# Third projection chunk with row blocks outermost, the token permutation beside it, and modulation sums two steps later

## The chip, the cores and the metric

The kernel runs on one core of a Trainium2 chip, as one launch. A core has TensorE (PE in the profile, with its weight loads as PEld), VectorE (DVE), ScalarE (ACT), GpSimd (POOL) and SyncE (SP, which here issues nearly all DMAs). Each engine works through its own queue in order and waits on semaphores for the others. The metric is device microseconds (us) of one execution, as the median of several runs; lower is better. A difference of under 0.2% (about 5.5 us here) is what a measurement of this kernel can't tell from no change.

## The reference

Two transformer-like blocks in float32 on 1024 tokens of width 1024 (8 tiles of 128 tokens), the first with 256 context tokens beside them (2 tiles). Only the head of the first block matters here:

```
mod   = silu(c) @ w_mod + b_mod                  # 6 x 1024 values
h     = rms_norm(x)   * norm1 * (1 + sc1) + sh1  # 1024 tokens
hc    = rms_norm(ctx) * norm1 * (1 + csc1) + csh1  # 256 context tokens
q_a, k_a, v_a, q_b, k_b, v_b = split(h @ w_in)   # and of hc @ w_in: k and v
q_a, k_a = rope(rms_norm(q_a)), rope(rms_norm(k_a))
q_b, k_b = rms_norm(q_b), rms_norm(k_b)
o_a = window attention(q_a, k_a, v_a, context)
o_b = 2-D neighbourhood attention(q_b, k_b, v_b, context)   # 16 rows x 64 columns of tokens
```

After it come the output projection, a gated feed-forward layer, a gated linear attention block and a second feed-forward layer with a convolution; none of these is touched.

## The kernel before, in words

Matrix products keep float32 accuracy by splitting each operand into a rounded part `hi` and a rest `lo` and adding three products: hi x whi, hi x wlo, lo x whi (`mm3`, lines 233 to 238; the loads of `hi`, `lo` are the stationary side, 128 x 128, and 256 weight columns stream through). The normalized tokens lie in `hT` (a `hi` and a `lo` tile, each 8 row blocks of 128 features x 1024 tokens) and those of the context in `hc`.

`w_in` is worked in nine chunks of 256 columns, list `P1C` (line 310), here called chunk 0 (`kva`), 1 and 2 (`qa`), 3 (`vb`), 4 and 5 (`kb`), 6 and 7 (`qb`), 8 (`vb`). The loop of lines 781 to 804 goes over chunks 2 to 8 and, inside, over token tiles `t`; `project` (line 716) runs 24 matmuls for one tile (8 row blocks x 3) into one of four PSUM buffers `acc`, and `evac` has ScalarE copy the sums to SBUF (line 629 or 617) and take four sums of squares of 64 columns (line 632). Beside each tile step three kinds of work are issued:

- `W.tick()` splits one quarter of the next chunk's weights (line 139 on ScalarE, 140 on VectorE) and, after the fourth, issues the next load;
- `do_later(2)` takes two items from the list `later`: for a chunk of queries or keys that is one `rsqrt` (11 small VectorE instructions, lines 248 to 261), and for each pair of tiles a `gain` (line 647 on VectorE, 649 on GpSimd), for `kva` and `qa` a `turn` (rotation, lines 518 to 523 on GpSimd and VectorE), and a `store` (a DMA, line 606);
- `mod_use()` adds one of 32 row blocks of `w_mod`, times one value of silu(c), to a sum `macc` on VectorE (lines 555, 557) and issues the load of a later block into one of three buffers `mraw` (line 537). Eight row blocks make one group of 1024 modulation values. With the next call after the eighth, `mod_row` has TensorE add `macc` over its 128 partitions (`pm`, line 580, two issues of 512 columns), VectorE add the bias (line 581), and with the call after that the row is stored.

Chunks 0 to 2 use the tokens in natural order. From chunk 3 on they must stand in strips of 8 columns of the 16 x 64 grid. `to_strips` (line 701), called between chunks 2 and 3, permutes `hT` in place: for each row block, ScalarE copies `hi` to an `mraw` buffer (line 709), GpSimd copies `lo` to a spare buffer (line 712), and VectorE writes both back in the new order (line 713, 16 instructions). Chunk 3 begins with the two context tiles, which are not permuted. SP issues the DMAs in program order; a spill that waits for a `turn` holds up the `mraw` loads behind it.

Of the kernel before, what the change touches and what calls it, by code (L numbers as in the profile page):

```python
# [9 lines left out]
F32 = mybir.dt.float32  # L10
R32 = mybir.dt.float32r
I32 = mybir.dt.int32
AF = mybir.ActivationFunctionType
# [5 lines left out]
P = 128  # L19
D = 1024  # L20
KD = 8
S = 1024
# [190 lines left out]
def kernel(ctx: ExitStack, tc: tile.TileContext, a: dict, out: bass.AP, dbg=None):  # L213
    nc = tc.nc
# [309 lines left out]


    mods = [(j, k) for j in range(4) for k in range(8)]
    mst = {"load": 0, "use": 0, "raw": {}}
    mpl = {}

    def mod_load():  # L530
# [8 lines left out]

    def mod_use():  # L540
        i = mst["use"]
        if i >= 34:
            return
        mst["use"] += 1
        for f in mst.pop("next", []):
            f()
        if i >= 32:
            return
        j, k = mods[i]
        r = mst["raw"].pop(i)  # L550
        if k == 0:
            mst["acc"] = mpl["p"].tile([P, 1024], F32, tag="macc", name="macc", bufs=2)
        m = mst["acc"]
        if k == 0:
            nc.vector.tensor_scalar(out=m, in0=r, scalar1=sil[:, k:k + 1], scalar2=None, op0=ALU.mult)
        else:
            nc.vector.scalar_tensor_tensor(
                out=m, in0=r, scalar=sil[:, k:k + 1], in1=m, op0=ALU.mult, op1=ALU.add)
        mod_load()
        if k == 5:  # L560
            mst["row"] = [mod_row_load(j, half) for half in range(2)]
        if k == 7:
            rows_ = mst.pop("row")
            mst["next"] = [lambda half=half: mod_row(j, half, m, rows_[half]) for half in range(2)]

    def row_view(n, k):
        o_ = voff[n] + k
# [6 lines left out]
            nc.sync.dma_start(out=row[:, 2], in_=row_view("norm2", 4 * half))  # L574
        return row

    def mod_row(j, half, m, row):
        c = slice(half * 512, half * 512 + 512)
        pm = ps_m.tile([P, 512], F32, tag="misc", name="pm", bufs=2)
        nc.tensor.matmul(pm[0:1, :], one1, m[:, c], start=True, stop=True)  # L580
        nc.vector.tensor_tensor(out=row[:, 0], in0=pm[0:1, :], in1=row[:, 1], op=ALU.add)
        if j == 2:
            nc.vector.scalar_tensor_tensor(out=row[:, 0], in0=row[:, 0], scalar=1.0,
                                           in1=row[:, 2], op0=ALU.add, op1=ALU.mult)

        def store():
            nc.sync.dma_start(out=dmod[j, c].rearrange("(o n) -> o n", o=1), in_=row[:, 0])

        mst.setdefault("next", []).append(store)

    def lhs(nm, t, k):
        if t >= 8:
            return [hc[i][:, k, (t - 8) * P:(t - 7) * P] for i in range(2)]
        return [hT[i][:, k, t * P:(t + 1) * P] for i in range(2)]
# [10 lines left out]
    def spill(dd, t, half, src):  # L605
        nc.sync.dma_start(out=dd[t:t + 2, :, half * 256:half * 256 + 256].rearrange("t p c -> p t c"), in_=src)

    def evac(ci, t, ps):
        nm, c0 = P1C[ci]
        half = {"kb": (c0 - 1280) // 256, "vb": (c0 - 1792) // 256, "qa": c0 // 256,  # L610
                "qb": (c0 - 768) // 256, "kva": 0}[nm]
        e = t % 2
        if nm == "vb":
            if e == 0:
                raws["v"] = p1.tile([P, 2, 256], F32, tag="vt", name="vt", bufs=2)
            vt = raws["v"]
            nc.scalar.activation(out=vt[:, e], in_=ps[:, :256], func=AF.Copy)
            if e == 1:
                spill(dvb, t - 1, half, vt)
            return  # L620
        nh = 2 if nm == "kva" else 4
        w = nh * 64
        nt_ = 10 if nm[0] == "k" else 8
        if t == 0:
            ss = p1.tile([P, 2, 40], F32, tag="hss", name="hss", bufs=4)
            raws[ci] = (KA if nm == "kva" else (p1 if ci in (1, 4, 6) else mpl["p"]).tile(
                [P, 10, 256], F32, tag="raw", name="raw"), ss)
        x, ss = raws[ci]
        nc.scalar.activation(out=x[:, t], in_=ps[:, 0:w], func=AF.Copy)
        for h in range(nh):  # L630
            sq = p1.tile([P, 64], F32, tag="hsq", name="hsq", bufs=2)
            nc.scalar.activation(out=sq, in_=ps[:, h * 64:h * 64 + 64], func=AF.Square,
                                 accum_out=ss[:, 0, t * nh + h:t * nh + h + 1])
        if nm == "kva":
            pv = ps[:, 128:256].rearrange("p (h d) -> p h d", h=2)
            nc.scalar.activation(out=VA[:, t, :, 0:64], in_=pv, func=AF.Copy)
            nc.vector.tensor_tensor(
                out=VA[:, t, :, 64:128], in0=pv, in1=VA[:, t, :, 0:64].bitcast(F32), op=ALU.subtract)
        if t < nt_ - 1:
            return  # L640
        gi = {"kva": 1, "kb": 3, "qa": 0, "qb": 2}[nm]
        last = {}

        def gain(t0):
            xx = x[:, t0:t0 + 2].rearrange("p t (h d) -> p (t h) d", d=64)
# [12 lines left out]
        def store(t0):  # L658
            src = last.get(t0, x[:, t0:t0 + 2])
            if nm == "kva":  # L660
                nc.vector.tensor_copy(out=x[:, t0:t0 + 2], in_=src)
            else:
                spill({"qa": dqa, "qb": dqb, "kb": dkb}[nm], t0, half, src)

        later.append(lambda: rsqrt(p1, ss[:, 1, :nt_ * nh], ss[:, 0, :nt_ * nh], nt_ * nh, 1.0 / 64))
        stages = [gain, turn, store] if nm in ("kva", "qa") else [gain, store]
        for i in range(nt_ // 2 + len(stages) - 1):
            for j, f in reversed(list(enumerate(stages))):
                t0 = 2 * (i - j)
# [28 lines left out]
            eng = nc.vector if t < 2 else nc.gpsimd  # L698
            eng.tensor_tensor(out=lo, in0=src, in1=hi.bitcast(F32), op=ALU.subtract)

    def to_strips():

        spare = p1.tile([P, 10, 256], F32, tag="raw", name="raw").rearrange("p a b -> p (a b)")
        for k in range(8):
            for i in range(2):
                h = hT[i][:, k]
                if i == 0:
                    tmp = mpl["p"].tile([P, 1024], F32, tag="mraw", name="mraw", bufs=3)
                    nc.scalar.activation(out=tmp, in_=h.bitcast(F32), func=AF.Copy)
                else:  # L710
                    tmp = spare[:, k % 2 * S:k % 2 * S + S]
                    nc.gpsimd.tensor_copy(out=tmp, in_=h.bitcast(F32))
                nc.vector.tensor_copy(out=h.rearrange("p (s r c) -> p s r c", s=8, c=8),  # L713
                                      in_=tmp.rearrange("p (r s c) -> p s r c", s=8, c=8))

    def project(ci, t):
        nm, c0 = P1C[ci]
        wi, wl = map(kc8, W.slots(ids["in", ci]))
        ps = ps_a.tile([P, 512], F32, tag="acc", name="pin", bufs=4)
        mm3(ps[:, :256], [(*lhs(nm, t, k), wi[:, k], wl[:, k]) for k in range(8)])  # L720
        evac(ci, t, ps)

# [58 lines left out]
    for ci, (nm, c0) in enumerate(P1C):  # L781
        if ci < 2:
            continue
        W.get(ids["in", ci])
        if ci == 3:
            to_strips()
            for _ in range(3):
                mod_load()
        ts = list(range(10 if nm in ("kb", "vb") else 8))
        for t in ts[8:] + ts[:8] if ci == 3 else ts:  # L790
            project(ci, t)
            if t >= 1:
                W.tick()
            do_later(2)
            if ci > 3 - (t > 1) and (t % 4 != 3 or ci == len(P1C) - 1):
                mod_use()
            if ci == len(P1C) - 1 and t == 5:
                do_later(99)
                while mst["use"] < 34:
                    mod_use()  # L800
                st_mod.close()
                qp = pool("q_raw", "left", stack=st_o)
                for x in range(3):
                    load_q(x)
# [1375 lines left out]
```

## Time and profile before

| | us |
|---|---|
| median of 3 runs | 2749.98 (2746.62 to 2752.45) |
| the profiled execution's own time | 2745.07 |
| its span on the core | 2743.1 |
| TensorE busy | 2583.6 (94% of the span) |
| VectorE busy | 1713.6 (62%) |
| ScalarE busy | 1053.2 (38%) |
| GpSimd busy | 1186.5 (43%) |

The projection stage lies between about 112 and 346 us of the span; the change is in it. TensorE is busy nearly throughout the kernel, so the places where it waits are looked for. Times in rows count from the start of the span. A matmul row's duration is that of its whole passage; matmuls overlap, and from one start to the next is the pace. A value in square brackets is idle time of the engine before the row, with what ended it. PEclk is the granted TensorE clock as a share of its upper level: 1.00 is 2.4 GHz, 0.50 is 1.2 GHz.

### The profile page before, as it was taken

To read this page: it belongs to the slowest core of one execution; us is meant where nothing else is said; L and a number is where in the kernel's file an instruction comes from. 1 tells how busy PE (TensorE), PEld (TensorE's weight loads), DVE (VectorE), ACT (ScalarE), POOL (GpSimd) and SP (SyncE) were. 2 spreads that over 40 slices of the span, in tenths; PEclk is the share of its full clock that TensorE was granted. 3 is DMA by queue.
4 is the path that set the end of the run, shared out by engine and by line. 5 is a ranking of instruction groups with operands and counts; after the bars stand their busy time and mean duration, and the time that the engine had idled before them with its cause. 6 is when DMAs were issued, how large, how long until landed. Compare 5 with 4: busy or idle time off the path is not lost. (4 is left out here: it accounts for less than half of the span.)

```text
span 2743.1 us, 37060 instructions
## 1 busy us (share of the span) xinstructions
PE 2583.6 (94%) x13861; PEld 2143.0 (78%) x13861; DVE 1713.6 (62%) x3361; ACT 1053.2 (38%) x2605; POOL 1186.5 (43%) x1079
## 2 busy tenths in 40 slices
PE   8969988888989999999999999999999999999998
PEld 4968977777987788888887868778777777777786
DVE  4585589999465555555564632422677777777766
ACT  4524377777232222222222542422443333333333
POOL 2462246677344677766662312121433333333321
PEclk9989999999999999999999999999999999999999
DMA  6145422220211111112112111111101111111112
GB/s 238 55 131 175 156 58 53 67 73 13 101 39 47 46 47 46 47 47 62 47 46 70 35 46 31 47 31 47 39 31 47 47 47 46 47 52 52 48 49 85
DMA packets 152540, 170.85 MB, mean 62 GB/s; under 512 B 39444, under 2 KB 135460, under 8 KB 151336
## 3 DMA queue, kind: packets, MB, share of 16 engines
q1 hardware_dynamic: 152200, 168.35, 19.4%
q8 instruction: 109, 1.79, 0.3%
q0 software_dynamic: 160, 0.14, 0.1%
q14 instruction: 71, 0.58, 0.1%
HBM read 154.81 MB, written 13.65 MB: 61 GB/s over the span
## 5 line engine op out<-in xcount | busy, mean ns | idle before, releaser
L140 POOL TENSOR_TENSOR wlo<-raw,whi 128x512 fp32r<-128x512 f32 x132 | 179.3, 1363 | 449.1 <-ACT whi L139 420.3
L1635 PE MATMUL pgu<-h,whi 128*128 128x512 f32 x864 | 342.4, 396 | 3.1 <-DVE h L1571 3.1
L1636 PE MATMUL pgu<-h,wlo 128*128 128x512 f32 x864 | 341.0, 395 | 0.5 <-POOL wlo L140 0.5
L1634 PE MATMUL pgu<-h,whi 128*128 128x512 f32 x864 | 341.3, 395 | 0.0
L140 DVE TENSOR_TENSOR wlo<-raw,whi 128x512 fp32r<-128x512 f32 (+2 forms) x304 | 232.2, 776 | 165.0 <-ACT whi L139 164.1
L139 ACT ACTIVATE whi<-raw 128x512 fp32r<-128x512 f32 (+1 forms) x436 | 232.2, 551 | 173.0 <-DMA raw<-in_w_down 60.9
L1653 DVE TENSOR_TENSOR uv<-pgu,uv 128x512 f32<-128x512 f32 x216 | 148.2, 686 | 149.8 <-PE pgu L1636 128.7
L237 PE MATMUL pdn<-wlo,hid 128*128 128x512 f32 x576 | 227.4, 395 | 12.3 <-DVE wlo L140 12.3
L236 PE MATMUL pdn<-whi,hid 128*128 128x512 f32 x576 | 226.5, 393 | 1.5 <-DVE uv L1362 1.1
L238 PE MATMUL pdn<-whi,hid 128*128 128x512 f32 x576 | 226.7, 394 | 0.0
L1363 POOL TENSOR_TENSOR x<-x,uv 128x512 f32<-128x512 f32 x144 | 192.2, 1356 | 31.6 <-DVE uv L1362 28.8
L1635 PEld LDWEIGHTS pgu<-h,whi 128*128 128x128 f32 x864 | 162.2, 188 | 42.2 <-DVE h L1571 3.6
L1634 PEld LDWEIGHTS pgu<-h,whi 128*128 128x128 f32 x864 | 162.4, 188 | 40.0
L1636 PEld LDWEIGHTS pgu<-h,wlo 128*128 128x128 f32 x864 | 162.2, 188 | 39.9 <-POOL wlo L140 0.9
L1504 POOL TENSOR_TENSOR hid<-sg,hid 128x512 fp32r<-128x512 f32 x80 | 106.9, 1341 | 193.7 <-ACT hid L1503 191.7
L1656 POOL TENSOR_TENSOR uv<-uv 128x512 f32<-128x512 f32 x72 | 106.2, 1475 | 163.8 <-DVE uv L1653 163.8
L236 PE MATMUL pin<-whi,h 128*128 128x256 f32 x576 | 167.5, 291 | 8.4 <-ACT whi L139 3.5
L238 PE MATMUL pin<-whi,h 128*128 128x256 f32 x576 | 168.1, 292 | 6.3 <-DVE h L713 6.1
L237 PE MATMUL pin<-wlo,h 128*128 128x256 f32 x576 | 166.7, 289 | 2.1 <-DVE wlo L140 2.1
L237 PEld LDWEIGHTS pdn<-wlo,hid 128*128 128x128 f32 x576 | 108.1, 188 | 41.9 <-DVE wlo L140 17.4
L1503 ACT ACTIVATE hid<-sg 128x512 fp32r<-128x512 f32 x80 | 50.3, 632 | 231.6 <-DVE sg L1501 231.6
L236 PEld LDWEIGHTS pdn<-whi,hid 128*128 128x128 f32 x576 | 108.2, 188 | 28.0 <-DVE uv L1362 1.5
(381 smaller groups left out, 7048.2 us busy)
## 6 DMA issues: line engine op xcount, KB each, us to landing
raw<-in_ffn_w_up SPq DMA_DIRECT2D x22, 1024.0 KB, 5.2
mraw<-in_w_mod SPq DMA_DIRECT2D x32, 512.0 KB, 4.1
raw<-in_w_gate SPq DMA_DIRECT2D x11, 1024.0 KB, 5.3
raw<-in_w_up SPq DMA_DIRECT2D x11, 1024.0 KB, 5.5
raw<-in_w_down SPq DMA_DIRECT2D x11, 1024.0 KB, 4.9
raw<-in_ffn_w_down SPq DMA_DIRECT2D x11, 1024.0 KB, 5.0
raw<-in_w_in SPq DMA_DIRECT2D x9, 1024.0 KB, 5.3
wm<-in_w_mod SPq DMA_DIRECT2D x8, 1024.0 KB, 13.1
```

The lines of the kernel that those rows point to most:

```text
L139: nc.scalar.activation(out=hi, in_=src, func=AF.Copy)
L140: (engine or self.engine or nc.vector).tensor_tensor(out=lo, in0=src, in1=hi.bitcast(F32), op=ALU.subtract)
L236: nc.tensor.matmul(ps, lh, rh, start=(i == 0), stop=False)
L237: nc.tensor.matmul(ps, lh, rl, start=False, stop=False)
L238: nc.tensor.matmul(ps, ll, rh, start=False, stop=(i == n - 1))
L1363: nc.gpsimd.tensor_tensor(out=xs, in0=xs, in1=tmp, op=ALU.add)
L1504: nc.gpsimd.tensor_tensor(out=hl[:, c], in0=sg[:, cc, c], in1=hh[:, c].bitcast(F32), op=ALU.subtract)
L1634: nc.tensor.matmul(ps, lh, rh, start=start and k == 0, stop=False)
L1635: nc.tensor.matmul(ps, lh, rl, start=False, stop=False)
L1636: nc.tensor.matmul(ps, ll, rh, start=False, stop=stop and k == n - 1)
L1653: nc.vector.tensor_tensor(out=o, in0=ps, in1=u, op=ALU.add)
L1656: nc.gpsimd.tensor_tensor(out=o, in0=u, in1=v, op=ALU.add)
```

## The change

It has four parts.

1. Chunk 2 no longer goes tile by tile. `to_strips(ci)` runs it with the row block `k` outermost: four PSUM buffers hold the sums of all eight tiles (two tiles per buffer), and for each `k` all eight tiles get their three matmuls. Before them ScalarE copies both parts of row block `k` into `mraw` buffers (three in all), and after them VectorE writes both back in strip order, so that row block `k` is permuted once chunk 2 has read it. GpSimd's copies and their spare buffer are gone. One weight quarter (from k = 1) and one `later` item are issued per `k`. After k = 7 all eight tiles are evacuated; their sums of squares become eight `later` items, read from SBUF.
2. In chunk 3 the two context tiles use the PSUM buffers `tp` (`early`) instead of `acc`.
3. `mod_use` is called in three of five tile steps instead of three of four.
4. `mod_row` runs with the second `mod_use` call after the group's last addition instead of the next one, and its store with the fourth instead of the second.

```
-        for f in mst.pop("next", []):
+        for f in mst["next"].pop(i, []):
...
-            mst["next"] = [lambda half=half: mod_row(j, half, m, rows_[half]) for half in range(2)]
+            mst["next"][i + 2] = [lambda half=half: mod_row(j, half, m, rows_[half], i + 4) for half in range(2)]
...
-    def to_strips():
+    def to_strips(ci):
+        wi, wl = map(kc8, W.slots(ids["in", ci]))
+        pss = [ps_a.tile([P, 512], F32, tag="acc", name="pin", bufs=4) for _ in range(4)]
+        pss = [pss[t // 2][:, t % 2 * 256:t % 2 * 256 + 256] for t in range(8)]
         for k in range(8):
+            tmp = []
             for i in range(2):
+                tmp.append(mpl["p"].tile([P, 1024], F32, tag="mraw", name="mraw", bufs=3))
+                nc.scalar.activation(out=tmp[i], in_=hT[i][:, k].bitcast(F32), func=AF.Copy)
+            for t in range(8):
+                hi, lo = lhs(P1C[ci][0], t, k)
+                nc.tensor.matmul(pss[t], hi, wi[:, k], start=(k == 0 and t % 2 == 0), stop=False)
+                nc.tensor.matmul(pss[t], hi, wl[:, k], start=False, stop=False)
+                nc.tensor.matmul(pss[t], lo, wi[:, k], start=False, stop=(k == 7 and t % 2 == 1))
+            for i in range(2):
+                nc.vector.tensor_copy(out=hT[i][:, k].rearrange("p (s r c) -> p s r c", s=8, c=8),
+                                      in_=tmp[i].rearrange("p (r s c) -> p s r c", s=8, c=8))
+            if k >= 1:
+                W.tick()
+            do_later()
+        for t in range(8):
+            evac(ci, t, pss[t], True)
...
-        if ci == 3:
-            to_strips()
+        if ci == 2:
+            to_strips(ci)
             for _ in range(3):
                 mod_load()
+            continue
...
-            if ci > 3 - (t > 1) and (t % 4 != 3 or ci == len(P1C) - 1):
+            if t % 5 in (0, 2, 4) or ci == len(P1C) - 1:
                 mod_use()
```

What moves, engine by engine. On TensorE the place is chunk 2; `pin` with a number is one PSUM buffer. Before, the end of its first tile and the begin of the second:

```order
L237 MATMUL pin_1237<-wlo_66,h1_0_279 128x256
L238 MATMUL pin_1237<-whi_65,h1_1_280 128x256
L236 MATMUL pin_1288<-whi_65,h1_0_279 128x256
L237 MATMUL pin_1288<-wlo_66,h1_0_279 128x256
L238 MATMUL pin_1288<-whi_65,h1_1_280 128x256
```

Now, the end of the first row block and the begin of the second:

```order
L723 MATMUL pin_1240<-whi_65,h1_1_280 128x256
L721 MATMUL pin_1237<-whi_65,h1_0_279 128x256
L722 MATMUL pin_1237<-wlo_66,h1_0_279 128x256
L723 MATMUL pin_1237<-whi_65,h1_1_280 128x256
L721 MATMUL pin_1238<-whi_65,h1_0_279 128x256
```

A buffer stood for 24 matmuls in a row before; now for 6 (the row for 1237 covers two tiles, each with its three), and all four are open until the chunk's end. The number of matmuls is the same.

On VectorE the place is the permutation; a CAST writes one part of one row block. Before, the last two of sixteen that stand in one block, and what follows:

```order
L713 CAST h_0_279<-mraw 128x1024
L713 CAST h_1_280<-raw 128x1024
L140 TENSOR_TENSOR wlo<-raw,whi 128x512
L647 TENSOR_TENSOR KA<-KA,hss 128x256
L661 COPY KA<-qr 128x256
L555 TENSOR_SCALAR macc<-mraw,sil 128x1024
```

Now, the two casts of one row block in chunk 2, between a `turn` and the next split and `gain`:

```order
L522 TENSOR_TENSOR qr<-raw,rope 128x8x16
L523 TENSOR_TENSOR qr<-qr,rp_1360 128x8x16
L725 CAST h_0_279<-mraw 128x1024
L725 CAST h_1_280<-mraw 128x1024
L140 TENSOR_TENSOR wlo<-raw,whi 128x512
L654 TENSOR_TENSOR raw<-raw,hss 128x512
```

The casts moved from one block between chunks 2 and 3 into pairs inside chunk 2, and both now read what ScalarE copied.

On TensorE the second place is the first modulation sum in chunk 4. Before, behind the tile of step t = 2:

```order
L238 MATMUL pin_2230<-whi_65,h1_1_280 128x256
L580 MATMUL pm_2266<-macc_1725,ones_72 1x512
L580 MATMUL pm_2269<-macc_1725,ones_72 1x512
L236 MATMUL pin_2276<-whi_65,h1_0_279 128x256
L237 MATMUL pin_2276<-wlo_66,h1_0_279 128x256
```

Now, behind the tile of step t = 5:

```order
L238 MATMUL pin_2286<-whi_65,h1_1_280 128x256
L580 MATMUL pm_2323<-macc_1657,ones_72 1x512
L580 MATMUL pm_2326<-macc_1657,ones_72 1x512
L236 MATMUL pin_2332<-whi_65,h1_0_279 128x256
L237 MATMUL pin_2332<-wlo_66,h1_0_279 128x256
```

The last addition to the group's `macc` was issued in step t = 1 of chunk 4 before, one tile ahead of the sum, and is in step t = 2 now, three tiles ahead. The other three sums moved in the same way: behind step t = 9 of chunk 5, t = 4 of chunk 7 and t = 5 of chunk 8 (before: t = 2 of chunk 5, t = 2 of chunk 6, t = 5 of chunk 7).

## Rows read from the trace of the kernel before

**Rows 1.** The page, section 1: busy time, share of span, instructions.

```profile
PE 2583.6 (94%) x13861; PEld 2143.0 (78%) x13861; DVE 1713.6 (62%) x3361; ACT 1053.2 (38%) x2605; POOL 1186.5 (43%) x1079
```

**Rows 2.** Waits of TensorE from 110 to 360 us: total, times, longest.

```profile
PE pm L580 <- DVE macc L557: 20.3, 4, 12.1
PE pin L238 <- DVE h L713: 6.1, 7, 2.2
```

**Rows 3.** Windows: stretch, its us, busy per engine (instructions), PEclk, DMA share, GB/s.

```profile
161.30:168.10 6.80, 6.74 (x29) 6.34 (x30) 6.66 (x21) 0.38 (x1) 0.91 (x2) 0.50 0.71 210
193.80:205.90 12.10, 0.00 (x0) 0.00 (x0) 10.80 (x18) 1.72 (x10) 10.26 (x14) 0.71 0.50 160
205.90:209.30 3.40, 3.37 (x5) 0.38 (x5) 1.25 (x2) 0.00 (x0) 0.00 (x0) 0.54 0.70 207
209.30:237.90 28.60, 28.60 (x241) 28.43 (x240) 14.61 (x23) 12.38 (x84) 3.15 (x2) 1.00 0.44 145
237.90:241.50 3.60, 0.04 (x1) 0.00 (x0) 3.60 (x5) 1.72 (x10) 2.31 (x2) 1.00 0.90 269
241.50:243.30 1.80, 1.75 (x4) 0.25 (x4) 1.80 (x2) 0.00 (x0) 1.12 (x1) 1.00 0.77 153
```

**Rows 4.** Timeline of TensorE around its two longest waits: start, us, what.

```profile
143.00 0.28 PE L238 MATMUL pin<-whi,hc 128*128 128x256 f32 x1
146.39 0.39 PE L236 MATMUL pin<-whi,h 128*128 128x256 f32 x1 [3.11 <-DVE h L713]
149.07 0.58 PE L238 MATMUL pin<-whi,h 128*128 128x256 f32 x1 [2.19 <-DVE h L713]
...
193.51 0.28 PE L238 MATMUL pin<-whi,h 128*128 128x256 f32 x1
205.93 3.41 PE L580 MATMUL pm<-macc,ones 128*1 128x512 f32 x4 [12.13 <-DVE macc L557]
```

**Rows 5.** Timeline of TensorE in chunk 2's first tile (granted clock 0.50).

```profile
114.03 0.41 PE L238 MATMUL pin<-whi,h 128*128 128x256 f32 x1
...
116.59 0.41 PE L238 MATMUL pin<-whi,h 128*128 128x256 f32 x1
```

**Rows 6.** Lines of the permutation: ns min/median/max, first and last start us.

```profile
L713 DVE CAST h<-mraw x8: 675/678/824, 145.5 to 161.2; 128x1024 fp32r<-128x1024 f32 x8
L713 DVE CAST h<-raw x8: 679/1522/1524, 147.5 to 161.8; 128x1024 fp32r<-128x1024 f32 x8
L709 ACT ACTIVATE mraw<-h x8: 1056/1058/1087, 138.7 to 155.8; 128x1024 f32<-128x1024 f32 x8
```

**Rows 7.** Timeline of VectorE: a root, a gain, a turn, a modulation step.

```profile
114.87 0.17 DVE L248 TENSOR_SCALAR rs_v<-hss 128x32 f32<-128x32 f32 x1
117.33 0.69 DVE L647 TENSOR_TENSOR raw<-raw,hss 128x512 f32<-128x512 f32 x1
...
164.71 0.68 DVE L140 TENSOR_TENSOR wlo<-raw,whi 128x512 fp32r<-128x512 f32 x1
...
180.49 0.69 DVE L647 TENSOR_TENSOR raw<-raw,hss 128x512 f32<-128x512 f32 x1
182.66 0.29 DVE L521 TENSOR_TENSOR rp<-raw,rope 128x128 f32<-128x128 f32 x1 [1.48 <-POOL raw L649]
184.95 1.48 DVE L557 SCALAR_TENSOR_TENSOR macc<-mraw,sil,macc 128x1024 f32<-128x1024 f32 x1
...
204.60 1.27 DVE L557 SCALAR_TENSOR_TENSOR macc<-mraw,sil,macc 128x1024 f32<-128x1024 f32 x1
```

**Rows 8.** Timeline of GpSimd: the last instruction of chunk 2's last turn.

```profile
204.07 0.46 POOL L520 TENSOR_TENSOR qr<-qr,rp 128x128 f32<-128x128 f32 x1
```

**Rows 9.** Timeline of ScalarE: one tile's evacuation, then a split.

```profile
129.12 0.39 ACT L629 ACTIVATE raw<-pin 128x256 f32<-128x256 f32 x1 [1.12 <-PE pin L238]
...
130.18 0.66 ACT L139 ACTIVATE whi<-raw 128x512 fp32r<-128x512 f32 x1
```

**Rows 10.** Timeline of SP: the first loads of queries for the attention stage.

```profile
335.73 3.16 SPq L778 DMA_DIRECT2D qraw<-dqa  x6
```

More of the change, by code (lines that the diff above doesn't have):

```diff
@@ L526 @@
     mods = [(j, k) for j in range(4) for k in range(8)]
-    mst = {"load": 0, "use": 0, "raw": {}}
+    mst = {"load": 0, "use": 0, "raw": {}, "next": {}}
     mpl = {}
@@ L541, in mod_use @@
         i = mst["use"]
-        if i >= 34:
+        if i >= 36:
             return
         mst["use"] += 1
-        for f in mst.pop("next", []):
+        for f in mst["next"].pop(i, []):
             f()
@@ L575, in mod_row_load, with mod_row @@
         return row
-    def mod_row(j, half, m, row):
+    def mod_row(j, half, m, row, at):
         c = slice(half * 512, half * 512 + 512)
@@ L587, in store @@
             nc.sync.dma_start(out=dmod[j, c].rearrange("(o n) -> o n", o=1), in_=row[:, 0])
-        mst.setdefault("next", []).append(store)
+        mst["next"].setdefault(at, []).append(store)
     def lhs(nm, t, k):
@@ L606, in spill, with evac @@
         nc.sync.dma_start(out=dd[t:t + 2, :, half * 256:half * 256 + 256].rearrange("t p c -> p t c"), in_=src)
-    def evac(ci, t, ps):
+    def evac(ci, t, ps, put_off=False):
         nm, c0 = P1C[ci]
@@ L629, in evac, with squares @@
         nc.scalar.activation(out=x[:, t], in_=ps[:, 0:w], func=AF.Copy)
[L630 to L633, printed above, removed]
+        def squares(src):
+            for h in range(nh):
+                sq = p1.tile([P, 64], F32, tag="hsq", name="hsq", bufs=2)
+                nc.scalar.activation(out=sq, in_=src[:, h * 64:h * 64 + 64], func=AF.Square,
+                                     accum_out=ss[:, 0, t * nh + h:t * nh + h + 1])
+        if put_off:
+            later.append(lambda: squares(x[:, t]))
+        else:
+            squares(ps)
         if nm == "kva":
@@ L699, in h_fm @@
             eng.tensor_tensor(out=lo, in0=src, in1=hi.bitcast(F32), op=ALU.subtract)
-    def to_strips():
-        spare = p1.tile([P, 10, 256], F32, tag="raw", name="raw").rearrange("p a b -> p (a b)")
+    def to_strips(ci):
+        wi, wl = map(kc8, W.slots(ids["in", ci]))
+        pss = [ps_a.tile([P, 512], F32, tag="acc", name="pin", bufs=4) for _ in range(4)]
+        pss = [pss[t // 2][:, t % 2 * 256:t % 2 * 256 + 256] for t in range(8)]
         for k in range(8):
+            tmp = []
@@ L705, in to_strips @@
             for i in range(2):
[L706 to L714, printed above, removed]
@@ L716, in project @@
-    def project(ci, t):
+                tmp.append(mpl["p"].tile([P, 1024], F32, tag="mraw", name="mraw", bufs=3))
[5 more added lines that the diff above has]
+                nc.tensor.matmul(pss[t], lo, wi[:, k], start=False, stop=(k == 7 and t % 2 == 1))
@@ L717, in project @@
+            for i in range(2):
[6 more added lines that the diff above has]
+            evac(ci, t, pss[t], True)
+    def project(ci, t, early=False):
         nm, c0 = P1C[ci]
         wi, wl = map(kc8, W.slots(ids["in", ci]))
-        ps = ps_a.tile([P, 512], F32, tag="acc", name="pin", bufs=4)
+        if early:
+            ps = ps_t.tile([P, 512], F32, tag="tp", name="pin", bufs=2)
+        else:
+            ps = ps_a.tile([P, 512], F32, tag="acc", name="pin", bufs=4)
@@ L784 @@
         W.get(ids["in", ci])
-        if ci == 3:
-            to_strips()
+        if ci == 2:
+            to_strips(ci)
             for _ in range(3):
                 mod_load()
+            continue
         ts = list(range(10 if nm in ("kb", "vb") else 8))
         for t in ts[8:] + ts[:8] if ci == 3 else ts:
-            project(ci, t)
+            project(ci, t, ci == 3 and t >= 8)
             if t >= 1:
@@ L798 @@
                 do_later(99)
-                while mst["use"] < 34:
+                while mst["use"] < 36:
                     mod_use()
```

## The prediction

> **What bounds the kernel now.** I read the page's busy times first: TensorE works in 94% of the span [rows 1], so only a wait of TensorE can be won back, and the edits touch one stage of it, from 113 to 346 us. The view of waits for that stretch shows who ends them: VectorE's modulation additions (20.3 us in four waits, one of 12.1) and VectorE's casts of the permuted tokens [rows 2]. The windows then give the price of work that doesn't wait: the ten tiles between the first two modulation sums ran 28.60 us for 240 matmuls at full clock, so 0.119 us a matmul and 2.86 us a tile; one modulation sum takes 1.8 us [rows 3]. With these two prices each stretch can be charged with what it should have taken:
>
> - The permutation. The second context tile of chunk 3 starts its last matmul at 143.00; the last matmul before the next long wait starts at 193.51 [rows 4]. Between them lie 11 tiles (eight of chunk 3, three of chunk 4), which cost 11 x 2.86 = 31.5 us; they took 50.5. Lost: 19.0. Part of it is waiting, row block by row block, for casts; part is the clock, which the windows show granted at 0.50 (1.2 GHz) from 161.3 to 168.1, behind that halting work [rows 3]. At that level a matmul takes (116.59 - 114.03)/12 = 0.213 us [rows 5].
> - The first modulation sum. TensorE stands for 12.1 us until the eighth addition has ended at 204.60 + 1.27 = 205.87 [rows 4, 7], and the sum then takes 3.4 us at a lower granted clock instead of 1.8 [rows 3]. Lost: 15.5 - 1.8 = 13.7.
> - The other three sums wait for 20.3 - 12.1 = 8.2 us together [rows 2]; the first of them is the window of 3.6 us, which left the clock at 1.00 [rows 3].
>
> Together 40.9 us. That is all that this change can win, since the number of matmuls and sums is the same.
>
> **The change part by part.** *Chunk 2 by row blocks.* TensorE's own cost is 192 matmuls as before, and none waits for a copy or a cast. It starts in the lower clock as before, ends a row block about every 2.86 us, the first near 117.6 and the last near 137.4. The context tiles (buffers `tp`, free then) cover 5.7 us more, to 143.2. Chunk 3's first permuted tile needs row block 7 only for its last three matmuls, at 143.2 + 7/8 x 2.86 = 145.7. So the question is whether VectorE has cast all blocks by 145.7.
>
> VectorE's queue from the first cast (117.7) to the last holds 16 casts, one root, four splits, three gains and two turns. A cast took 0.68 us, or 1.52 while GpSimd worked on the same tokens; the last two start 0.6 apart, at 161.2 and 161.8, so a row's duration overlaps the next by some 0.07 [rows 6]. GpSimd now does no copies, only the gains and turns, so I take six of the sixteen at 1.45 and ten at 0.61: 14.8. Root 117.33 - 114.87 = 2.5, gains 3 x 0.69, splits 4 x 0.6, turns 2 x (184.95 - 182.66 = 2.3) [rows 7]: 11.6. Sum 26.4, end 144.1, 1.6 us before the deadline. If every cast took 1.45 the end would be 152.5, and TensorE would lose 6.8 us and some clock; if none did, casts would follow each row block and end by 139. I take no wait, with 0 to 10 us as bounds. ScalarE has, per row block, two copies of 1.06 [rows 6] and up to one split of 0.66 [rows 9], 2.8 against 2.86; the copies go ahead only as casts free one of three buffers, and the last waits for the cast of block 6, so they are not later than VectorE. The eight evacuations after it (without squares 0.3 to 0.4 each) free the buffers two by two while TensorE is on the context tiles. Win: 19.0, at worst 9.
>
> The Trainium skill ("SBUF — State Buffer", Who interferes with whom) says that VectorE and GpSimd share a port pair as an exclusive lock and that the loser blocks for the whole instruction. The rows agree in kind: 0.68 against 1.52 for the same cast. As an estimate by that rule alone, one cast of each pair could wait out a GpSimd instruction, which is the bound of 152.5 above rather than 144.1.
>
> *The squares put off.* Their 32 small instructions move into chunk 4's first four steps, where ScalarE has one evacuation with squares (130.18 - 129.12 = 1.06 [rows 9]), eight squares of under 0.2 (what 1.06 leaves beside the copy, over four) and one split of 0.66: 3.3 against 2.86 for three steps. Four sum buffers hide that lag of 1.5 us. Cost 0; without that cover 1.5.
>
> *The sums later.* Before, VectorE went from its last cast (161.8 + 0.68 = 162.5 [rows 6]) to the end of the eighth addition (205.87) in 43.4 us. Now that stretch holds one gain and two turns of `qa` instead of four and four (three gains 2.7, two turns 4.6, three waits for GpSimd of about 1.3 go: 11.2), and gains one split, one small gain and one small turn (2.3): 34.5. From 144.1 that is 178.6. TensorE reaches the first sum after 8 + 6 tiles: 143.2 + 40.0 = 183.2. So the wait goes, with 4.6 us to spare; a tenth more VectorE time eats most of it. Win 13.7, at worst 8. The other three sums stand three to four tiles (8.6 to 11.4 us) behind their last addition instead of one, more than the 3.6 to 3.7 that was missing. Win 8.2, at worst 4.
>
> *What is late next.* Only eight `later` items go in chunk 2 instead of sixteen, and eight squares are new, so the rotation of chunk 2's queries ends in the last step of chunk 4. Chunk 5's first evacuation writes the buffer that this rotation reads, and ScalarE stands there until it ends. After the eighth addition VectorE has two splits and a root (3.8), then four gain-and-turn stages, which run at GpSimd's pace: from 180.49 to 204.07 + 0.46 = 204.5, 24.0 us [rows 7, 8]. So 178.6 + 3.8 + 24.0 = 206.4, and with one evacuation (1.06) the first sum buffer is free at 207.5. TensorE needs it for the fifth tile of chunk 5, at 183.2 + 1.8 + 8 x 2.86 = 207.9. That is a tie. Step by step, with the bias rows of the sum in between (1.4), it comes 3 us late. I take 2 us, bounds 0 and 10, the second sum included, which is as close behind VectorE. ScalarE's splits queue behind that wait, but chunk 6's weights have all of chunk 5.
>
> *Mod steps at three of five tiles* take as much VectorE time in all; more of it lies in chunk 8, where VectorE has room. The last sum now falls in chunk 8's step t = 5, ahead of the first loads of queries. These were issued at 335.73 [rows 10], some 10 us before they are used, so about 4 us of delay stay hidden; cost 0, at most 2.
>
> Sum: 40.9 - 2 = 38.9 us. Against the profiled execution's own 2745.07 that gives 2706.2. That execution lies 4.9 under the median of the runs shown, 2749.98; on the median it is 2711.
>
> **The rivals.**
>
> 1. *VectorE and GpSimd become the bound.* For it: the deadlines above are met by 1.6, 4.6 and 0.4 us in a queue of some 90 us that is nearly free of gaps. Against it: each wait of TensorE gives the queue that time back, so the misses don't add. With a tenth more time over the queue, 9 us late and 3 to 5 of lost clock: 12 to 14 more, 2724.
> 2. *The permutation stays on the path*, so the change does only half of what it says: ScalarE's copies, held by three buffers, and the casts run behind TensorE by most of chunk 2. Then only the sums' 21.9 is won: 2728. Against it, the load of 26.4 us in 27 us of time.
> 3. *Matmuls that change their sum buffer every six run at half clock.* If the granted clock fell to 0.50 for chunk 2, each of 192 matmuls would take 0.213 instead of 0.119: 18 us back, 2729. The rows speak against it: ten tiles, with a change of buffer after each, kept 28.60 us and a clock of 1.00 [rows 3]. The Trainium skill ("TensorE: Matmul & The Clock Gate", A second HAM failure mode: psum-queue depth-cycling) reports a kernel in which cycling through banks made TensorE idle briefly and its clock oscillate; no run here shows that yet.
> 4. *Slower: the open sum buffers stall TensorE.* Four buffers, two tiles in each, are open at once; if a matmul that changes tiles must wait for the one before to drain, starts move from 0.119 to the full passage. At the 0.28 of a passage [rows 4] that is 31 us lost, still a gain of 8; it is a loss from 0.35 a matmul on (44.4/192 = 0.23 more), and at the 0.39 of a first matmul after a wait [rows 4] it is 52 lost: 2763. Nothing in the rows shows such a drain.
>
> **How the numbers follow.** The forecast has 0.64, rival 1 0.20, rival 2 0.06, rival 3 0.05, rival 4 0.05. The predicted time is the forecast's, 2711; its own range, with the worst of the single bounds and none, is 2704 to 2720. Rivals 1 to 3 reach 2736, so the range is 2703 to 2736. A change under 0.2%, 5.5 us, can't be told from none. Faster than that: the forecast, rivals 1 to 3, together 0.95, less 0.02 for what I have not seen: 0.93. Rival 4 between its two ends: 0.03 same, 0.04 slower.
>
> **What would show it.** Right: TensorE without a wait for the casts from 143 to 166 and without half clock there; no wait of a sum over 1 us; chunk 8's last matmul starting near 307 instead of 346; casts of chunk 2 partly at 0.68. Wrong: a wait of chunk 3's matmuls for the casts, or of chunk 5's fifth tile for ScalarE, of more than 5 us; starts in chunk 2 more than 0.12 us apart after 117; a stage after 346 that takes longer than before.

## The result

The changed kernel takes 2705.53 us (median of four, 2705.16 to 2706.59), the kernel before 2748.30 (2745.10 to 2752.45): a ratio of 0.9844, 95% interval 0.9827 to 0.9861, so 43 us faster. The forecast was 2711. The changed kernel was timed twice more beside the experiments: 2711.33 (0.9868, 0.9852 to 0.9885) and 2711.17 (0.9870, 0.9853 to 0.9887). By these 36 us is the fairer figure; the last section says how far the other 6 are explained.

### The profile page after: what moved, and what is told of

It reads as the page before. It is cut to its first block, busy times and chain, and to the rows that moved or that the text cites. A ratio compares the mean times of both kernels' runs of the same rounds, so it can differ in the third digit from the quotient of the medians.

```text
span 2704.8 us, 37053 instructions
## 1 busy us (share of the span) xinstructions
PE 2569.5 (95%) x13861; PEld 2135.2 (79%) x13861; DVE 1713.1 (63%) x3361; ACT 1060.6 (39%) x2613; POOL 1187.3 (44%) x1071
## 3 DMA queue, kind: packets, MB, share of 16 engines
q8 instruction: 109, 1.79, 0.3%
## 5 line engine op out<-in xcount | busy, mean ns | idle before, releaser
L236 PE MATMUL pin<-whi,h 128*128 128x256 f32 x512 | 146.1, 285 | 5.8 <-ACT hsq L634 2.1
L237 PE MATMUL pin<-wlo,h 128*128 128x256 f32 x512 | 146.1, 285 | 1.7 <-DVE wlo L140 1.7
L238 PE MATMUL pin<-whi,h 128*128 128x256 f32 x512 | 146.1, 285 | 0.2 <-DVE h L706 0.2
L237 PEld LDWEIGHTS pdn<-wlo,hid 128*128 128x128 f32 x576 | 108.1, 188 | 42.0 <-DVE wlo L140 17.6
```

The source lines that it names most:

```text
L236: nc.tensor.matmul(ps, lh, rh, start=(i == 0), stop=False)
L237: nc.tensor.matmul(ps, lh, rl, start=False, stop=False)
L238: nc.tensor.matmul(ps, ll, rh, start=False, stop=(i == n - 1))
```

## The profile after

The page's busy times, which answer to [rows 1]; the span went from 2743.1 to 2704.8 us:

```profile
PE 2569.5 (95%) x13861; PEld 2135.2 (79%) x13861; DVE 1713.1 (63%) x3361; ACT 1060.6 (39%) x2613; POOL 1187.3 (44%) x1071
```

TensorE runs as many matmuls in 14 us less busy time (the granted clock was 0.50 for 34.1 us of the stage before, for 6.8 now) and waits less. The waits of TensorE from 110 to 360 us, against [rows 2] (total, times, longest):

```profile
PE pin L236 <- ACT hsq L634: 2.1, 1, 2.1
...
PE pin L721 <- ACT whi L139: 1.5, 1, 1.5
...
PE pm L580 <- DVE macc L557: 0.7, 1, 0.7
```

The casts are gone from the list; the four waits of the sums, 20.3 us, are one of 0.7; the first row is new and is the one that the prediction announced for chunk 5's fifth tile. The windows (columns as in [rows 3]; the count takes in instructions that only reach into a window) show both long stretches without a pause, and the clock around the new wait:

```profile
118.10:143.50 25.40, 25.40 (x216) 25.40 (x215) 24.64 (x46) 17.75 (x27) 13.46 (x16) 1.00 0.33 102
143.50:183.20 39.70, 39.70 (x337) 39.62 (x335) 32.91 (x88) 19.50 (x125) 17.74 (x30) 1.00 0.68 208
...
208.10:210.20 2.10, 0.00 (x0) 0.00 (x0) 2.07 (x4) 1.25 (x10) 2.02 (x3) 1.00 0.12 41
210.20:213.60 3.40, 3.40 (x16) 3.40 (x17) 3.02 (x13) 3.40 (x23) 0.23 (x2) 0.50 0.52 130
```

The first is chunk 2 from just behind the start of its second row block, with the context tiles: 0.119 us from start to start at full clock (214 starts from 118.10 to 143.41), though the buffer changes every six. VectorE is full there (24.64 of 25.40). The second holds the 14 tiles up to the first sum. TensorE's timeline at the places of [rows 4]:

```profile
112.66 0.38 PE L721 MATMUL pin<-whi,h 128*128 128x256 f32 x1 [1.46 <-ACT whi L139]
...
183.05 0.28 PE L238 MATMUL pin<-whi,h 128*128 128x256 f32 x1
183.26 0.59 PE L580 MATMUL pm<-macc,ones 128*1 128x512 f32 x1
...
210.20 0.58 PE L236 MATMUL pin<-whi,h 128*128 128x256 f32 x1 [2.14 <-ACT hsq L634]
...
296.27 0.59 PE L580 MATMUL pm<-macc,ones 128*1 128x512 f32 x1 [0.73 <-DVE macc L557]
...
309.43 0.28 PE L238 MATMUL pin<-whi,hc 128*128 128x256 f32 x1
```

The first sum follows the last matmul with no wait where [rows 4] has 12.13. Chunk 8's last matmul starts at 309.43; in the kernel before it is this one:

```profile
345.81 0.28 PE L238 MATMUL pin<-whi,hc 128*128 128x256 f32 x1
```

VectorE, against [rows 6, 7]: two undisturbed pairs of casts, the last pair, then the eighth addition, a split that waits for ScalarE, the root and first gain of chunk 2's queries, and the end of the second group; behind them the gain of GpSimd that the last pair of casts meets:

```profile
117.60 1.30 DVE L725 CAST h<-mraw 128x1024 fp32r<-128x1024 f32 x2 [2.46 <-PE pin L722]
...
139.29 1.29 DVE L725 CAST h<-mraw 128x1024 fp32r<-128x1024 f32 x2
...
141.10 2.39 DVE L725 CAST h<-mraw 128x1024 fp32r<-128x1024 f32 x2
...
178.63 1.28 DVE L557 SCALAR_TENSOR_TENSOR macc<-mraw,sil,macc 128x1024 f32<-128x1024 f32 x1
...
181.53 0.69 DVE L140 TENSOR_TENSOR wlo<-raw,whi 128x512 fp32r<-128x512 f32 x1 [1.62 <-ACT whi L139]
182.47 0.18 DVE L248 TENSOR_SCALAR rs_v<-hss 128x32 f32<-128x32 f32 x1 [0.25 <-ACT hsq L634]
...
185.42 0.69 DVE L654 TENSOR_TENSOR raw<-raw,hss 128x512 f32<-128x512 f32 x1
...
224.93 3.50 DVE L557 SCALAR_TENSOR_TENSOR macc<-mraw,sil,macc 128x1024 f32<-128x1024 f32 x2
```

```profile
141.26 1.68 POOL L656 TENSOR_TENSOR raw<-raw,qg 128x512 f32<-128x512 f32 x1 [2.76 <-DVE raw L654]
```

The casts end at 143.49, ahead of the 145.9 at which TensorE (chunk 3's first permuted tile starts at 143.4) comes to row block 7. The rotation's last read of the raw buffer (L519) and its last instruction, where [rows 8] has 204.07, then, in ScalarE's timeline, the evacuation of chunk 5 that waits for that read:

```profile
208.41 0.50 POOL L519 TENSOR_TENSOR qr<-raw,rope 128x128 f32<-128x128 f32 x1
208.99 1.32 POOL L520 TENSOR_TENSOR qr<-qr,rp 128x128 f32<-128x128 f32 x1
```

```profile
208.94 0.38 ACT L629 ACTIVATE raw<-pin 128x256 f32<-128x256 f32 x1 [11.00 <-POOL qr L519]
```

ScalarE stands for 11.0 us; four sum buffers hide all but 2.14 of it.

## The experiments

All are compared by the stage: from the start of chunk 2's first matmul to that of chunk 8's last, read from each profile's TensorE timeline. "Waits" are the sum of TensorE's idle gaps of over 0.5 us in it; the difference of the two columns is work and clock. Each row is one profile; the changed kernel's three lie 1.8 us apart, so smaller differences of the stage say nothing.

| kernel | stage | waits | stage less waits | median us |
|---|---|---|---|---|
| before | 233.3 | 29.5 | 203.8 | 2744.9 to 2748.3 |
| changed (its three profiles) | 196.8, 195.1, 195.0 | 2.9, 4.1, 4.1 | 193.9, 191.0, 191.0 | 2705.5, 2711.3, 2711.2 |
| strips_only | 219.8 | 21.5 | 198.2 | 2730.4 |
| sums_only | 219.5 | 15.9 | 203.6 | 2729.1 |
| no_early | 202.7 | 7.3 | 195.4 | 2717.1 |
| raw_halves | 196.8 | 4.5 | 192.3 | 2714.1 |
| halves_sum3 | 193.3 | 0.7 | 192.5 | 2706.2 |
| cast_twice | 200.6 | 6.4 | 194.2 | 2713.1 |
| no_casts | 194.2 | 3.3 | 190.9 | 2704.3 |
| spill_act | 195.7 | 3.3 | 192.4 | 2707.3 |
| squares_direct | 207.8 | 14.0 | 193.7 | 2719.3 |
| halves_sum3_act | 192.8 | 0.7 | 192.1 | 2703.4 |

The three profiles without any half clock in the stage (the changed kernel's second and third, and no_casts) agree on 191.0 within 0.1: that is the stage's work at full clock. What a row has above that is clock.

**One half of the change each.** Strips_only is the changed kernel with these lines as before (and the bound on the calls of `mod_use` at 34 again):

```
-            mst["next"][i + 2] = [lambda half=half: mod_row(j, half, m, rows_[half], i + 4) ...]
+            mst["next"][i + 1] = [lambda half=half: mod_row(j, half, m, rows_[half], i + 2) ...]
-            if t % 5 in (0, 2, 4) or ci == len(P1C) - 1:
+            if ci > 3 - (t > 1) and (t % 4 != 3 or ci == len(P1C) - 1):
```

> Chunk 2 by row blocks as in the changed kernel; the modulation sums as before (next call, three of four tiles). Theory A: the wait of the first sum was VectorE's backlog behind the casts, so it goes with the casts and not with the later issue. VectorE's last cast ends at 143.5 us, its eighth addition some 34 us later, 177.6; TensorE is there after 11 tiles, 143.4 + 31.5 = 174.9: the first sum waits about 3 us instead of 12.1, the other three keep about 8; of the 42.8 us between the medians some 27 are won, 2721 us. Theory B, as the prediction's sum has it (terms that add): only the permutation's 19 are won, about 2730 us, and the first sum still waits about 12.

Sums_only is the kernel before with `mod_use` at three of five tiles from chunk 3 on and `i + 2`, `i + 4` for the sums and their store (bound 36).

> The kernel before, with only the sums issued two steps later and three of five tiles. Theory A: VectorE's backlog stays, so the later sum meets a later eighth addition: 205.9 + about 5 to 7 us of gains and turns of one more step, against TensorE at 193.8 + 3 x 2.86 = 202.4; the first sum still waits 9 to 11 us, the other three stop waiting (8.2): about 10 won, 2738 us. Theory B (terms that add): 13.7 + 8.2 = 21.9 won, 2726 us, no sum waits over 1 us.

Measured: 0.9948 (0.9933 to 0.9963) and 0.9945 (0.9930 to 0.9961), so 13.6 and 13.8 us of stage, where both together give 36.6. Neither theory holds; the 2730 us of strips_only are theory B's number, but not for its reason, since the first sum waits 4.2 us there and not 12. TensorE's timeline of strips_only at its first two sums:

```profile
177.55 3.57 PE L580 MATMUL pm<-macc,ones 128*1 128x512 f32 x4 [4.15 <-DVE macc L557]
...
223.59 3.57 PE L580 MATMUL pm<-macc,ones 128*1 128x512 f32 x4 [12.80 <-DVE macc L557]
```

The first sum did what theory A said (the eighth addition ended at 177.5, forecast 177.6; 4.2 of wait, forecast about 3). But the time came back at the second, which waits 12.8 us where it waited 3.6 before [rows 3]: the second group ends at 223.5, and TensorE, now early, asks at 210.8. In the changed kernel that group ends no earlier, at 228.4; TensorE asks only at 229.0. In sums_only the first sum still waits, half as long:

```profile
PE pin L238 <- DVE h L713: 6.1, 7, 2.2
PE pm L580 <- DVE macc L557: 6.0, 1, 6.0
```

So the first half makes TensorE early, and the second lets VectorE be late; each is worth 23 us beside the other (219.8 and 219.5 against 196.8) and 14 alone.

**The context tiles' own buffers.**

```
-            project(ci, t, ci == 3 and t >= 8)
+            project(ci, t)
```

> The changed kernel, with chunk 3's context tiles in the four open buffers instead of two of their own. Theory: TensorE stands at 137.7 us until ScalarE has evacuated two tiles, 141.6: 3.9 us, and up to 3 us of half clock behind it; 4 of these come back because chunk 5's fifth tile then comes too late to wait (2.1 us and 1.6 of clock there): 0 to 4 us slower, 2706 to 2710. Rival, nothing comes back: 7 slower, 2712. Rival, the buffers are free in time: the same as the changed kernel.

```profile
140.56 0.58 PE L236 MATMUL pin<-whi,hc 128*128 128x256 f32 x1 [4.05 <-ACT raw L629]
```

The wait is the one expected. The stage is 5.9 to 7.7 us longer than the changed kernel's, the time 2717.14 (0.9898, 0.9882 to 0.9913): nearer to the rival. Chunk 5's wait shrank only to 1.5, since the rotation came later too. The `tp` buffers are a working part of the change.

**The new wait taken away.** Raw_halves makes the raw buffer two tiles, so that chunk 5 waits for half of the rotation at a time:

```
...
+                part = [pl.tile([P, n, 256], F32, tag=f"raw{n}", name="raw") for n in (4, 6)]
...
```

> The changed kernel, with the buffer of raw queries and keys as two tiles (token tiles 0 to 3 and 4 to 9), so that chunk 5's first evacuation waits only for the first half of chunk 2's rotation, which ends near 199 us, and its fifth for the rest, 210. Theory: the 2.1 us wait of chunk 5's fifth tile goes, and the 1.6 us of half clock behind it: 3.7 faster, about 2702 us. Rival: VectorE's and GpSimd's queue is the bound, and the wait comes back at the next sum or the next weights: 0 to 1 faster.

TensorE's waits, then the end of VectorE's second group:

```profile
PE pm L580 <- DVE macc L557: 4.5, 2, 3.7
```

```profile
225.05 3.47 DVE L557 SCALAR_TENSOR_TENSOR macc<-mraw,sil,macc 128x1024 f32<-128x1024 f32 x2
```

The rival is right. Chunk 5's wait is gone, and 3.7 us stand at the second sum, because VectorE ends that group at 228.5 whether TensorE waits in chunk 5 or not (228.4 above). The median, 2714.1, lies above all three of the changed kernel; behind the stage this profile took 2392 us. Halves_sum3 adds `i + 3` and `i + 5` for the sums:

> The changed kernel, with the raw buffer as two tiles and each sum issued with the third use after the last addition instead of the second. Theory: VectorE's queue is the bound up to the second group's last addition, 228.4 us whatever TensorE waits for; with the first evacuation free and the second sum one tile later (about 228 us) no wait over 1 us is left in chunks 4 to 6: the stage takes 193 us against 196.8, the time 3 to 4 us less than the changed kernel's on this chip. Rival: the wait finds the next place (the third sum, the weights of chunk 6): 196 to 197 us again.

The stage is 193.3 with one wait of 0.7 us left, as the theory had it; 2706.20 (0.9853, 0.9839 to 0.9868) against 2711.33 (0.9868, 0.9852 to 0.9885) for the changed kernel on the same chip, a difference that the intervals don't separate. The changed kernel's expectation was:

> The changed kernel itself, to have it on the same chip as the next three. The stage from chunk 2's first matmul to chunk 8's last took 196.8 us in its first profile, with half clock from 114.6 to 118.1 and from 210.2 to 213.6; 195 to 197 us again, and about 2706 us in all, if the clock's drops after the stage fall as they did (2386 us after the stage, against 2387 to 2392 in the other runs).

The stage came out as expected, at 195.1; the time after it did not: 2394 us, not 2386 (from the start of chunk 8's last matmul to the end of the program's last).

**Is VectorE the bound?** More and less of its work in chunk 2. Cast_twice:

```
-            for i in range(2):
+            for i in (0, 0, 1):
                 nc.vector.tensor_copy(out=hT[i][:, k].rearrange("p (s r c) -> p s r c", s=8, c=8),
```

> The changed kernel, with the first of the two casts of each row block done twice: eight more VectorE instructions of 0.65 to 1.2 us. Theory: VectorE's last cast ends 8 us later, 151.5 instead of 143.5, against 145.9 at which TensorE needs it: 5 to 6 us of wait and up to 3 of half clock there, and the second group's last addition moves from 228 to 236: the stage takes 8 to 12 us more, 205 to 209. Rival: VectorE has room for it (it is busy 63% of the span): 0 to 2 us more.

No_casts leaves out these lines and the copies, so the permutation is missing and the tokens stay in natural order:

> The changed kernel without the permutation: ScalarE's sixteen copies and VectorE's sixteen casts are left out, so the tokens stay in natural order. Theory: their 18 us of VectorE go from its queue; TensorE then waits for nothing in the stage but the first weights: 2.1 + 1.7 us at chunk 5 and 0.7 at the fourth sum go, 192 to 193 us against 196.8. Rival: the casts and copies also slow TensorE's matmuls while they run: under 190. Rival: the wait at chunk 5 is ScalarE's and GpSimd's alone: 196 to 197.

The last block of cast_twice on VectorE, and where TensorE waits for it:

```profile
145.32 3.25 DVE L725 CAST h<-mraw 128x1024 fp32r<-128x1024 f32 x3
```

```profile
145.95 0.39 PE L236 MATMUL pin<-whi,h 128*128 128x256 f32 x1 [2.91 <-ACT raw L629]
```

The casts end 5.4 us later (148.6 against 143.2), less than I expected because the extra casts were cheap. The stage is 5.5 longer, but not one for one: 2.3 are waits (6.4 against 4.1), and 3.2 are clock, of two spells of half clock (from 146.7 and 215.0, 3.4 us each) that the profile it is compared with doesn't have. What is shown is that 5.4 us more of VectorE make TensorE stand 2.9 us where it did not. The wait is not that for row block 7: ScalarE's last copies stand behind the casts, and its evacuations behind the copies, so a sum buffer is not free. Without any casts, though, nearly nothing is won in the stage: 0.9 us against the changed kernel's 195.1 on the same chip. (The medians, 2704.3 and 2711.3, differ by 7; the profiles differ by 8 behind the stage, 2386 against 2394 us, where the programs are the same.) VectorE's queue of no_casts around the eighth addition tells why:

```profile
173.70 0.69 DVE L140 TENSOR_TENSOR wlo<-raw,whi 128x512 fp32r<-128x512 f32 x1 [0.31 <-ACT whi L139]
177.19 0.69 DVE L140 TENSOR_TENSOR wlo<-raw,whi 128x512 fp32r<-128x512 f32 x1 [2.80 <-ACT whi L139]
177.80 1.28 DVE L557 SCALAR_TENSOR_TENSOR macc<-mraw,sil,macc 128x1024 f32<-128x1024 f32 x1
```

VectorE is 3 us early and then waits for ScalarE's split; the addition ends at 179.1 instead of 179.7.

**Is ScalarE, then?** Spill_act issues chunk 3's spills of values from ScalarE's queue:

```
...
-                spill(dvb, t - 1, half, vt)
+                spill(dvb, t - 1, half, vt, nc.scalar if ci == 3 else nc.sync)
```

> The changed kernel, with chunk 3's spills of values issued from ScalarE's queue instead of SP's. Leaving out all casts moved the eighth addition by under 1 us, so VectorE's backlog can't be what sets it. Theory: ScalarE does. It stands 12.6 us in two waits for spills that SP issues late (behind loads that wait for VectorE's additions), and VectorE's splits and chunk 2's squares come late behind that. With the spills on their own queue these waits go, the eighth addition ends 2 to 4 us earlier (176 to 178), the rotation of chunk 2 starts 2 to 3 us earlier, and chunk 5's wait of 2.1 to 2.4 us goes or falls under 0.5: the stage takes 2 to 4 us less. Rival: the transfer itself is what takes long, or VectorE is the bound after all: eighth addition at 179 to 180 and the stage 195 to 197 as now.

ScalarE's waits from 143 to 183 us of the changed kernel, then of spill_act:

```profile
ACT vt L617 <- DMA dvb<-vt: 12.3, 2, 6.3
```

```profile
ACT vt L617 <- DMA dvb<-vt: 2.5, 1, 2.5
```

Ten of the 12 us went, and the eighth addition stayed, as the rival had it: 179.6 in both kernels on that chip. In this run VectorE does not wait for the split; its own queue ends at the same moment. Chunk 5's wait fell from 2.4 to 1.6. So two chains tie within 1 us there: VectorE's queue from the casts on and ScalarE's from the first tile of chunk 4 on (steps of 3.0 to 3.5 us against TensorE's 2.86: evacuation, eight late squares, split). Taking work off one shows only the other. Squares_direct undoes the putting off:

```
-            evac(ci, t, pss[t], True)
+            evac(ci, t, pss[t])
```

> The changed kernel, with chunk 2's squares taken at its evacuation as before and not put off. Theory: the evacuation takes 8 x 1.06 = 8.5 us instead of 2.3, which the context tiles hide; but the root, two gains and a turn or two of chunk 2's queries then come ahead of the eighth addition on VectorE, some 8 to 11 us: the first sum waits 4 to 6 us and half clock costs 1.7 behind it, chunk 5's wait of 2.1 to 2.4 goes: the stage takes 2 to 5 us more. Rival: putting them off bought nothing, and the earlier rotation only removes chunk 5's wait: 2 us less.

```profile
PE pm L580 <- DVE macc L557: 11.8, 2, 11.0
```

The direction is right, the size is not: 12.8 us more stage, for 2 to 5 expected. The root, gains and turns came ahead of the eighth addition, which ended at 197.3; I had allowed 8 to 11 us for them, and it was 17.6: three gains and two turns stand ahead of it on VectorE, where I counted two and one or two, and the keys' last copy before them ended 6.0 us later (179.67 against 173.72 on the same chip) already. VectorE's timeline shows where that comes from:

```profile
150.79 0.69 DVE L140 TENSOR_TENSOR wlo<-raw,whi 128x512 fp32r<-128x512 f32 x1 [7.16 <-ACT whi L139]
```

This is the first split behind the casts. ScalarE does its part of it only at 150.07, behind eight evacuations with their squares (141.13 to 149.80), where the changed kernel does it at 143.16 and VectorE waits 0.60. The context tiles hide the long evacuation from TensorE, as expected, but not from VectorE.

**Both repairs and the spills.**

> Raw buffer as two tiles, sums with the third use, and chunk 3's spills on ScalarE's queue. Theory: with no wait over 1 us left in the stage beside the first weights, the spills add nothing measurable to the version without them: stage 191 to 193.5, the time 3 to 6 us under the changed kernel's on this chip. Rival: the spills' issue costs ScalarE time that shows in a wait of TensorE: 1 to 3 us more than that.

> The changed kernel itself, on the same chip as the next three: 2705 to 2712 us, the stage 195 to 197.

2703.43 us (2699.81 to 2705.90; 0.9841, 0.9824 to 0.9859) against 2711.17 (2708.45 to 2713.39; 0.9870, 0.9853 to 0.9887) for the changed kernel on the same chip. It has the lowest median of all versions, but lies only 2.1 us under the changed kernel's first series. The stage, 192.8, is as expected. The stage's windows, the changed kernel (third) and this one:

```profile
112.60:309.80 197.20, 191.20 (x1555) 183.72 (x1556) 155.63 (x291) 93.22 (x473) 87.79 (x92) 1.00 0.57 176
```

```profile
112.90:306.20 193.30, 192.05 (x1552) 184.82 (x1552) 158.70 (x290) 93.40 (x468) 94.24 (x92) 0.99 0.57 179
```

TensorE is busy for 192.05 of 193.30 us, though this profile, unlike the other, had half clock at the start, which took 1.5 us back. Of the 7.7 us, 3.3 are waits that are gone; the profiles differ behind the stage too (2386 against 2394 us), where the programs are the same, and what of the 7.7 comes from there can't be credited to the edits.

## Why the prediction was right, point by point

- *The permutation, 19.0.* From 143.5 to the first sum there is neither a wait nor a low clock, 14 tiles in 39.7 us; 11 of them take 31.2, for 50.5 before, so 19.3 won. Right. VectorE's casts ended at 143.49, forecast 144.1: eight pairs took 14.2 us, for 14.8. The total was right with another make-up: three casts of 1.8 us, two of 0.95 and eleven of 0.7, not six of 1.45 and ten of 0.61. (The half clock before lasted from 147.6 to 168.1 and not only from 161.3; the sum doesn't change by it.)
- *The first sum, 13.7.* Right: no wait, full clock. The eighth addition ended at 179.9, forecast 178.6; TensorE came at 183.26, forecast 183.2.
- *The other three, 8.2.* All but the 0.73 at the fourth (and, in the second and third profile, 0.97 and 0.98 at the second). The fourth was misread: it stands two tiles behind its last addition (steps t = 3 and t = 5 of chunk 8), not three to four, and waited 0.90 before.
- *The wait at chunk 5, 2.* It came where it was put, at 2.14 us, and in this profile half clock followed for 3.4, which costs 3.4 x (1 - 0.119/0.213) = 1.5 more that the sum doesn't have. The size is in part luck. I put the squares at cost 0 and had the rotation start at 178.6 + 3.8 = 182.4. The first gain came at 185.42: the eighth addition ended 1.3 late, and behind it VectorE stood 1.62 us for a split of ScalarE and 0.25 for the late squares. ScalarE was behind because it had stood for a spill until 168.29, and because eight late squares took 1.9 us, 0.24 each, where I had under 0.2. So the rotation ended at 210.3 instead of 206.4. That step failed. Against it, ScalarE did not wait for the rotation's end, as I had it, but for its last read of the buffer, and went on at 208.94. The two errors partly cancel, and the 2 was picked between a tie and my own step-by-step count of 3.
- *The modulation steps, cost 0.* Right. The first loads of queries were issued 10.3 us ahead of chunk 8's last matmul, before 10.1 [rows 10]:

```profile
299.18 3.16 SPq L798 DMA_DIRECT2D qraw<-dqa  x6
```

- *The sum, 38.9.* By these, 19.3 + 13.7 + 7.5 - 3.6 = 36.9; the stage got shorter by 36.6. The profiled execution won 38.5 (2745.07 to 2706.59), about 2 more, behind the stage. That the total lies within 0.4 of the forecast is so far luck. The upper end of the range, 2736, is worked out nowhere: rivals 1 to 3 are priced at 2724 to 2729.
- *A sign of being wrong that appeared.* The prediction named a longer time after the stage as one. It was 2388 us before, 2386 in the first profile of the changed kernel and 2394 in the other two. The programs are the same there, and most other versions took 2386 to 2389 (raw_halves 2392), so no run ties it to the change, and none rules that out.
- *That the terms add.* They do for the whole change, and not for its halves (13.6 and 13.8). The sum was read from waits that were all removed together; it did not say that the later sums are what pays for the earlier tokens. The prediction's own remark that misses don't add has this other side: gains of one alone are taken back.
- *Rival 1*, VectorE the bound: not the case at the price given, but its edge is where the kernel now stands. Casts that end 5.4 us later bring a wait of 2.9 us and half clock behind it, and the second group's end at 228 sets what can be won in chunk 5. With the raw buffer and the sums changed too, waits of TensorE fall to 0.7 us.
- *Rival 2*: no wait for the casts, so no. *Rivals 3 and 4*: 0.119 us a matmul and a granted clock of 1.00 in chunk 2 refute both. The Trainium skill ("TensorE: Matmul & The Clock Gate", A second HAM failure mode: psum-queue depth-cycling) tells of a kernel in which cycling through banks made TensorE idle briefly and its clock oscillate. A change every six matmuls, with four buffers open, is not such a case here: 25.4 us without idle time or a lower clock.
- *The shared port.* The prediction's bound of 152.5 has every cast at 1.45; one slow cast of each pair, which it names as the ground for that bound, gives 8 x 1.45 + 8 x 0.61 + 11.6 = 28.1, an end at 145.8. The end was 143.49, because only three of the eight pairs met a gain of GpSimd (2.39 to 2.40 us); one met a rotation (1.82), and four met nothing (1.28 to 1.30). In each of the three the gain began while the first cast ran and took 1.68 us instead of 1.29, and the second cast ended 0.55 us after the gain (143.49 against 141.26 + 1.68 = 142.94). The Trainium skill ("SBUF — State Buffer", Who interferes with whom) says that the loser of the shared port pair blocks for the whole instruction; the trace agrees, since the second cast ends as if it had begun only when the gain was done.

## What to carry to other kernels

A wait that an engine ends is a debt of that engine: move the waiting work forward alone, and the debt is asked for at the next place. Ask, for each wait that you remove, when the same engine is due next; here 23 of the 36.6 us hung on asking VectorE later as well as giving it less to do at the wrong time. And where taking away a whole job from an engine changes nothing, look for a second chain that ends at the same time before calling the first one free: doubling half of the job made TensorE wait at once.

## What the runs showed of the hardware

- Whether the clock drops after a wait is not settled by the wait's length: behind the same 1.46 us ahead of chunk 2 the granted clock went to 0.50 for 3.4 us in seven of the fourteen profiles of this case, and behind 2.1 to 2.4 us at chunk 5 in the changed kernel's first profile but not in its second and third. Ahead of chunk 2 it went with what had been: from 40 to 119 us every profile has 10.2 us of half clock, and the drop behind the wait came in just the seven that had had only 6.8 of it by 66 us. So a stage can look 1.5 us longer for a spell that another profile had before it.
- The same instructions after the stage took 2386 us in the first profile of the changed kernel and 2394 in the other two. TensorE's waits there were 97.6, 99.6 and 100.4 us and its half clock 45.9, 62.3 and 58.1 us. At the rate above, waits and clock together make 9.2 and 8.2 us for the 8.3 and 7.5 measured. Half clock alone doesn't give the time: sums_only had 59.7 us of it with 93.9 us of waits, and took 2387. Why the spells fall differently stays open. This is of the size of the spread between 2705.5 and 2711.3, and more than some of the steps studied here.
- A pair of casts of 128x1024 took 1.30 us alone and 2.39 beside GpSimd's gain: the first cast kept its 0.69, the gain went from 1.29 to 1.68, and the second cast from 0.69 to 1.79.
